# Low part of the transposed attention weights multiplied with the values' high part alone (128 columns in place of 256), in a hybrid decoder block on one core

## The chip, the cores and the metric

The kernel runs on one core of a Trainium2 chip. The metric is the device time of one execution in microseconds (us); lower is better. Five engines work side by side on a core and wait for each other by semaphores: PE (TensorE, matmuls; its weight loads are listed apart as PEld), DVE (VectorE), ACT (ScalarE), POOL (GpSimd), and SP, which here only issues DMAs.

## The reference

One decoder block over 1024 tokens of width 1024. A projection gives a pooled branch, queries, keys and values of four heads, and two gates. What the change touches is the differential attention: two softmax maps per head, one subtracted from the other, multiplied with the values.

```python
def block(args):
    qa, qb, start = args
    ...
    def probs(qq, kk):
        s = jnp.einsum('bhqd,bhkd->bhqk', qq, kk).astype(jnp.float32) * scale + bias
        s = jnp.where(causal, s, -jnp.inf)
        return jax.nn.softmax(s, axis=-1)

    a = probs(qa, k1) - lam * probs(qb, k2)
    return jnp.einsum('bhqk,bhkd->bhqd', a.astype(vh.dtype), vh)
...
m = jax.nn.sigmoid(gate_a) * ya + jax.nn.sigmoid(gate_b) * yb
h = h + rms_norm(jnp.einsum('bsd,de->bse', m, w_out), mix_post_g)
```

Everything is float32. After this comes a SwiGLU feed-forward part of 2816 hidden units, which the change leaves alone.

## The kernel before

PE multiplies in a reduced 32-bit format (fp32r), so each float32 operand is kept as two parts: `hi`, rounded, and `lo`, the rest. A product normally takes three matmuls (hi with hi, hi with lo, lo with hi): this is `triple` (lines 800 to 802). The big projections use a seven-product scheme of Strassen's kind over blocks of 512 columns.

The kernel is one program in this order: norm and projections (queries, keys, values, pooled branch, gates); the region of the mixer (function `mixer`, line 240), which holds attention, both branch products and the gating; the output projection (tiles `wo`, lines 1260 to 1262); the feed-forward part. Intermediate results go through DRAM and come back by DMA.

In the mixer, four heads times eight query blocks of 128 rows (32 rows in all) are worked off, each in three steps:

- `scores` (line 424) multiplies a query block (`QA`, `QB`: its two parts) with the keys `K` into a PSUM tile `s`, for both maps; DVE adds the distance bias and takes the minimum for the exponent (`E`, line 452), ACT takes the exponential, DVE combines the two maps into one `E` (line 466).
- `transposes` (line 471) turns each 128x128 block of `E` on PE into `aT`, up to four blocks in a PSUM bank; ACT writes the high part `AT[:, 0]` (line 484) and DVE the low part `AT[:, 1]` (line 656).
- `values` (line 492) is where the change lies. For query block `qb` it goes over key blocks `b` = 0 to `qb`. The stationary operand is a 128x128 block of `AT`, first its high part, then its low part; the moving operand is 256 columns, the 128 columns of the values' high part and beside them the 128 of their low part. Both go into 256 columns of one PSUM tile `o`. ACT takes the right half times the reciprocal of the sum (line 509), and DVE adds the left half to it (line 511), giving `O`. So the left half of `o` holds hi and lo of the weights over the values' high part, and the right half the same over the values' low part.

A head has 1+2+...+8 = 36 such blocks, four heads 144, so 288 matmuls of 256 columns.

Between these steps PE does *filler* work: the last projection products, and `block` (line 397 and after), which multiplies the branch weights (`wb_hi`, `wb_lo`) with the pooled branch (`y2h`, `y2l`; the results are copied to `ma`) or, when attention is done, with the normalised and turned attention output (`OTh`, `OTl`). For the latter the gates come by DMA into `sgs`; DVE multiplies `ma` with one half, and the block's result with the other, and adds.

The order of all this on each engine is not written by hand. `mixer` describes every step as an operation with an engine, a cost in microseconds, what it reads and writes, and a rank; `Plan.schedule` (line 144) is a list scheduler that goes through them by these costs, with the number of buffers in `CAPS` (two PSUM banks each for `mm`, which `aT` and `o` share, `fil` for branch blocks and `pair` for `s` and `oT`). The program is then issued in the planned order, and the semaphores hold the true dependencies. So a changed cost in one operation can move any operation of the region on any engine.

Of the kernel before, what the change touches and what calls it, by code (L numbers as in the profile page):

```python
# [16 lines left out]
P = 128  # L17
# [222 lines left out]
def mixer(pl, k):  # L240
# [11 lines left out]
    def bank(pool, s):  # L252
        return pl.tile(pool, lambda: getattr(k, pool)(s))
# [7 lines left out]
    def mac(o, l, r, start, stop, skip=False):  # L261
        nc.tensor.matmul(o, l, r, start=start, stop=stop, skip_group_check=skip)  # L262
# [129 lines left out]
    def block(t, hi, lo, i, mov, rank):  # L392
        o = bank("fil", "branch")
        for q in range(4):
            mh, ml = mov[q // 2]

            def fn(q=q, mh=mh, ml=ml):
                c = slice(i * P, (i + 1) * P)
                k.triple(o(), hi()[:, q, c], lo()[:, q, c], mh()[:, q % 2, half(t)], ml()[:, q % 2, half(t)],
                         q == 0, q == 3, False)  # L400
            pl.op("PE", TRIPLE, fn, r=[hi, lo, (mh, (q % 2, t)), (ml, (q % 2, t))], w=[o], rank=rank + q * .01, chain="fill")
        return o
# [6 lines left out]
    n = 0  # L409
    for d in range(0, KD, 2):  # L410
        hi, lo = branch_weights(0, d, lambda: k.w_branch_a, -3.0 + 4 * n / 3)
        for i in range(2):
            for t in range(2):
                o = block(t, hi, lo, i, y2, 2000.0 + n)
                m, c = ma[t][(d + i) // 4], (d + i) % 4
                pl.op("ACT", act(HALF), lambda m=m, c=c, o=o: A.copy(m()[:, c, :], o()), r=[o], w=[(m, c)],
                      rank=URGENT)
# [74 lines left out]
    def values(h, qb):  # L492
        Vt = heads[h][3]
        ats, rec = attends[h, qb]
        r0 = pos[h, qb]
        o = bank("mm", "o")
        for b0 in range(0, qb + 1, 4):
            n = min(4, qb + 1 - b0)

            def fn(b0=b0, n=n):  # L500
                vv = Vt().rearrange("p i (b d) -> p b i d", b=NB)
                for b in range(b0, b0 + n):
                    for j in range(2):
                        mac(o()[:, :2 * P], ats[b // 4]()[:, j, b % 4 * P:(b % 4 + 1) * P], vv[:, b, :, :],
                            b == 0 and j == 0, b == qb and j == 1)
            last = pl.op("PE", n * .24, fn, r=[ats[b0 // 4], Vt], w=[o], rank=r0)
        row_done.append(last)
        ov = lambda: O[h]()[:, qb, :]
        pl.op("ACT", .368, lambda: A.mul(ov(), o()[:, P:2 * P], rec()[:, 0:1]), r=[o, rec], w=[(O[h], qb)],
              rank=r0 - 1.5)  # L510
        pl.op("DVE", .346, lambda: V.scalar_tensor_tensor(out=ov(), in0=o()[:, :P], scalar=rec()[:, 0:1], in1=ov(),
                                                         op0=ALU.mult, op1=ALU.add), r=[o, rec],
              w=[(O[h], qb)], rank=r0 - 1.5)
        pl.op("ACT", .5, lambda: k.sumsq(ov(), oss[h]()[:, qb:qb + 1]), r=[(O[h], qb)], w=[(oss[h], qb)],
              rank=r0 - .5)
# [32 lines left out]
    for i in range(-AHEAD, len(seq)):  # L548
        j = i + AHEAD
        if j < len(seq):  # L550
            h, at = divmod(j, len(QORDER))
            if at == 2 and 0 < h < NH - 1:
                heads[h + 1] = (*load_qk(h + 1, i), *load_bv(h + 1, i))
            scores(*seq[j])
        if 0 <= i + 1 < len(seq):
            transposes(*seq[i + 1])
        if i >= 0:
            values(*seq[i])
            h, at = divmod(i, len(QORDER))
            if h < NH - 1 and at == len(QORDER) - 1:  # L560
                head_norm(h, list(range(NB)), i + 1.5)
            elif h == NH - 1 and at < NH - 1:
                for t in range(2):
                    turn_head(at, t, i + .5)
            elif h == NH - 1 and at % 4 == 3:
                head_norm(h, list(range(4, 8) if at == 3 else range(4)), i - 2.0)
                turn_head(h, 1 if at == 3 else 0, i - 1.0)
# [3 lines left out]
    for n, (d, t) in enumerate(order):  # L571
        if d not in ws:
# [4 lines left out]
        r0 = len(seq) + n  # L577
# [4 lines left out]
              r=[(sg, 0)], w=[(m, c)], rank=r0 + 2, port=True)  # L582
        if (1, d) in (k.unfinished if k else [(1, 6), (1, 7)]):
            pl.op("ACT", act(HALF) + .2, lambda sg=sg: A.activation(sg()[:, 1], sg()[:, 1], AF.Sigmoid),
                  w=[(sg, 1)], rank=r0)
        o = block(t, hi, lo, i, OT, 3000.0 + n)
        pl.op("DVE", dve(HALF), lambda o=o, sg=sg: tt(sg()[:, 1], o(), sg()[:, 1], ALU.mult), r=[o],
              w=[(sg, 1)], rank=URGENT)
        pl.op("DVE", dve(HALF), lambda m=m, c=c, sg=sg: tt(m()[:, c, :], m()[:, c, :], sg()[:, 1], ALU.add),
              r=[(sg, 1)], w=[(m, c)], rank=r0 + 1, port=True)  # L590

    wo = []
    for kp in range(4):
        hi, lo = a8([P, 2, D], F32R, "woh"), a8([P, 2, D], F32R, "wol")
        for j in range(2):
            kb = 2 * kp + j
            raw = wpt("wraw", [P, D], F32, "wo_raw")
            rank = len(seq) + 8.0 + kb
            dma(lambda raw=raw: raw(), lambda kb=kb: k.w_out[kb * P:(kb + 1) * P, :], rank, 0.52, w=[raw])
            pl.op("ACT", 1.06, lambda hi=hi, j=j, raw=raw: A.copy(hi()[:, j, :], raw()), r=[raw], w=[(hi, j)],  # L600
                  rank=rank)
            pl.op("DVE", 1.23, lambda hi=hi, lo=lo, j=j, raw=raw: k.sub(lo()[:, j, :], raw(), hi()[:, j, :]),
                  r=[raw, (hi, j)], w=[(lo, j)], rank=rank, port=True)
# [1020 lines left out]
```

## Time and profile before

| | us |
|---|---|
| median of 3 runs | 1257.43 |
| lowest and highest | 1257.41, 1257.58 |
| the profiled execution | 1257.79 |
| its span in the profile | 1255.9 |

The span runs from the first to the last instruction; 1.9 us lie around it. The granted clock of PE was 0.999 of full speed. Rows of the profile name the engine, the line of the kernel, the operation and the tiles (`o<-V,AT` writes `o` and reads `V` and `AT`), the shape and a count. In a timeline the first column is the start in microseconds from the start of the span and the second the duration; a number in square brackets is idle time of the engine ahead of the row, with what ended it. PE's matmuls overlap: what one costs in a stream is the distance from its start to the next start, not its duration.

### The profile page before, as it was taken

The numbers are of one execution on the slowest core, as the hardware profiler recorded it, in microseconds if no ns is written. First come the engines' busy times: TensorE is split into PE (matmuls) and PEld (weight loads), VectorE is DVE, ScalarE is ACT, GpSimd is POOL, SyncE is SP. The second block draws the span as 40 slices with busy tenths as digits, with TensorE's granted clock in tenths as the row PEclk, the third lists the DMA queues.
The fourth block names the chain that finished last, engine by engine and source line by source line (L and its number), as shares of the span: only waits on it lengthen the run. The fifth ranks groups of instructions, "written<-read, shape, count | busy, mean of one in ns | idle before, by whom it ended". The sixth has DMA issues, their size and how long they took to land.

```text
span 1255.9 us, 15668 instructions
## 1 busy us (share of the span) xinstructions
PE 1240.8 (99%) x5912; PEld 1040.8 (83%) x5912; DVE 835.3 (67%) x1296; ACT 578.3 (46%) x1039; POOL 144.2 (11%) x128
## 2 busy tenths in 40 slices
PE   8999999999999999999999999999999999999997
PEld 7878888888899998888888888888888888888886
DVE  5976775435498789755697655645655536965666
ACT  7543344434477774344553333333333333454552
POOL 4100000000201100010102111111111012000222
PEclk9999999999999999999999999999999999999999
DMA  8475336333692117523314332223322358733236
GB/s 253 149 233 192 138 120 224 109 122 118 233 370 102 51 51 276 177 101 118 120 57 126 126 112 98 92 95 108 126 101 88 122 195 275 250 110 106 80 108 210
DMA packets 137243, 183.34 MB, mean 146 GB/s; under 512 B 7376, under 2 KB 90064, under 8 KB 134736
## 3 DMA queue, kind: packets, MB, share of 16 engines
q1 hardware_dynamic: 124448, 147.61, 35.8%
q10 hardware_dynamic: 12720, 34.74, 7.3%
q8 instruction: 46, 0.75, 0.2%
q14 instruction: 29, 0.24, 0.1%
HBM read 124.39 MB, written 57.93 MB: 145 GB/s over the span
## 4 chain that ended last, share of the span: by engine, by line
PE 94%; DVE 2%; ACT 1%; issue 1%; POOL 1%; DMA 1%; SPq 0%; POOLq 0%; DVEq 0%; ACTq 0%
PE Y L800 10%; PE Y L801 10%; PE Y L802 10%; PE X L800 5%; PE X L801 5%; PE X L802 5%; PE Yd L800 3%; PE Yd L802 3%; PE Yd L801 3%; PE s L262 3%; PE Z L801 3%; PE Z L802 3%; PE Z L800 3%; PE o L262 3%; PE branch L800 2%; PE branch L801 2%
## 5 line engine op out<-in xcount | busy, mean ns | idle before, releaser
L729 DVE TENSOR_TENSOR p<-Z,p 128x512 f32<-128x512 f32 x34 | 23.5, 690 | 160.8 <-PE Z L802 157.1
L801 PE MATMUL Y<-A_lo,Wh 128*128 128x512 f32 x296 | 115.4, 390 | 0.3 <-DVE A_lo L656 0.3
L800 PE MATMUL Y<-A_hi,Wh 128*128 128x512 f32 x296 | 115.4, 390 | 0.0
L802 PE MATMUL Y<-A_hi,Wl 128*128 128x512 f32 x296 | 115.0, 389 | 0.0
L800 PE MATMUL Y<-S_hi,Wh 128*128 128x512 f32 x280 | 109.2, 390 | 0.7 <-ACT p L836 0.7
L800 PE MATMUL X<-S_hi,Wh 128*128 128x512 f32 x280 | 109.2, 390 | 0.0
L801 PE MATMUL Y<-S_lo,Wh 128*128 128x512 f32 x280 | 109.1, 389 | 0.0
L802 PE MATMUL Y<-S_hi,Wl 128*128 128x512 f32 x280 | 109.0, 389 | 0.0
L801 PE MATMUL X<-S_lo,Wh 128*128 128x512 f32 x280 | 108.9, 389 | 0.0
L802 PE MATMUL X<-S_hi,Wl 128*128 128x512 f32 x280 | 108.9, 389 | 0.0
L769 ACT CAST Wh<-wf_t 128x1024 fp32r<-128x1024 f32 x70 | 72.7, 1052 | 71.4 <-PE X L801 30.0
L656 DVE TENSOR_TENSOR Wl<-wf_t,Wh 128x1024 fp32r<-128x1024 f32 x70 | 87.0, 1250 | 6.2 <-ACT Wh L769 6.2
L769 ACT CAST Wh<-w_raw 128x1024 fp32r<-128x1024 f32 x72 | 60.6, 843 | 65.4 <-PE Z L801 38.1
L656 DVE TENSOR_TENSOR w_op<-wd,w_op 128x512 fp32r<-128x512 f32 x77 | 56.5, 734 | 48.4 <-ACT w_op L733 48.4
L733 ACT CAST w_op<-wd 128x512 fp32r<-128x512 f32 x77 | 47.9, 622 | 73.1 <-PE Yd L802 34.6
L656 DVE TENSOR_TENSOR Wl<-w_raw,Wh 128x1024 fp32r<-128x1024 f32 x72 | 69.1, 960 | 14.8 <-ACT Wh L769 14.7
L800 PE MATMUL Yd<-w_op,s_op 128*128 128x512 f32 x176 | 68.6, 390 | 0.0
L801 PE MATMUL Yd<-w_op,s_op 128*128 128x512 f32 x176 | 68.5, 389 | 0.0
L802 PE MATMUL Yd<-w_op,s_op 128*128 128x512 f32 x176 | 68.3, 389 | 0.0
L729 DVE TENSOR_TENSOR wf_t<-w_raw,wf_t 128x512 f32<-128x512 f32 x70 | 65.7, 938 | 1.1
L801 PEld LDWEIGHTS Y<-A_lo,Wh 128*128 128x128 f32 x296 | 55.6, 188 | 12.1 <-DVE A_lo L656 0.7
L800 PEld LDWEIGHTS Y<-A_hi,Wh 128*128 128x128 f32 x296 | 55.6, 188 | 11.8 <-DVE p L729 0.3
(274 smaller groups left out, 3055.9 us busy)
## 6 DMA issues: line engine op xcount, KB each, us to landing
s_raw<-fsd SPq DMA_DIRECT2D x35, 512.0 KB, 3.6
w_raw<-in_w_in_dram SPq DMA_DIRECT2D x32, 512.0 KB, 4.1
w_raw<-in_w_ffn_gate_dram SPq DMA_DIRECT2D x22, 512.0 KB, 3.7
w_raw<-in_w_ffn_up_dram SPq DMA_DIRECT2D x22, 512.0 KB, 3.7
fsd<-fss SPq DMA_DIRECT2D x11, 1024.0 KB, 3.9
wd<-in_w_ffn_down_dram SPq DMA_DIRECT2D x44, 256.0 KB, 5.6
fsd<-F SPq DMA_DIRECT2D x33, 256.0 KB, 2.3
qd<-qk_st ACTq DMA_DIRECT2D x16, 512.0 KB, 4.0
```

Of the source, the lines that this page charges most:

```text
L262: nc.tensor.matmul(o, l, r, start=start, stop=stop, skip_group_check=skip)
L656: nc.vector.tensor_tensor(out=o, in0=a, in1=f32(hi), op=ALU.subtract)
L729: nc.vector.tensor_tensor(out=o, in0=a, in1=b, op=op)
L733: nc.scalar.copy(hi, a)
L769: nc.scalar.copy(hi, a)
L800: nc.tensor.matmul(o, ah, bh, start=start, stop=False, skip_group_check=goes_on)
L801: nc.tensor.matmul(o, ah, bl, start=False, stop=False, skip_group_check=goes_on)
L802: nc.tensor.matmul(o, al, bh, start=False, stop=stop, skip_group_check=goes_on)
```

## The change

In `values`, the low part of the weights is multiplied with the values' high part alone. The product of the two low parts, which the right half of `o` held beside the rest, is left out. For every block after the first the narrow matmul now comes ahead of the wide one. The cost that the planner is told per block goes from 0.24 to 0.231 us, and the whole region is planned anew.

```diff
@@ -500,10 +500,10 @@
                 for b in range(b0, b0 + n):
-                    for j in range(2):
-                        mac(o()[:, :2 * P], ats[b // 4]()[:, j, b % 4 * P:(b % 4 + 1) * P], vv[:, b, :, :],
-                            b == 0 and j == 0, b == qb and j == 1)
-            last = pl.op("PE", n * .24, fn, r=[ats[b0 // 4], Vt], w=[o], rank=r0)
+                    for j in (1, 0) if b else (0, 1):
+                        mac(o()[:, :(2 - j) * P], ats[b // 4]()[:, j, b % 4 * P:(b % 4 + 1) * P],
+                            vv[:, b, :2 - j, :], b == 0 and j == 0, b == qb and j == (0 if b else 1), True)
+            last = pl.op("PE", n * .231, fn, r=[ats[b0 // 4], Vt], w=[o], rank=r0)
```

PE has as many matmuls as before; where eight of one shape stood in a row, shapes now alternate. PE's order in the first row of attention, before (`s` scores, `o` weights times values, `aT` a transpose; the numbers tell tiles apart):

```order
L262 MATMUL s_2946<-K_2155,QB_2738 128x384
L262 MATMUL o_2958<-V_2772,AT_2894 128x256 x8
L482 MATMUL aT_2970<-ident,E_2845 128x128
L262 MATMUL o_2958<-V_2772,AT_2919 128x256 x8
L262 MATMUL s_2985<-K_2155,QA_2154 128x384
```

The second half of the same row in the change:

```order
L482 MATMUL aT_2970<-ident,E_2845 128x128
L262 MATMUL o_2958<-V_2772,AT_2919 128x128
L262 MATMUL o_2958<-V_2772,AT_2919 128x256
L262 MATMUL o_2958<-V_2772,AT_2919 128x128
L262 MATMUL o_2958<-V_2772,AT_2919 128x256
L262 MATMUL o_2958<-V_2772,AT_2919 128x128
L262 MATMUL o_2958<-V_2772,AT_2919 128x256
L262 MATMUL o_2958<-V_2772,AT_2919 128x128
L262 MATMUL o_2958<-V_2772,AT_2919 128x256
L262 MATMUL s_2985<-K_2155,QA_2154 128x384
```

Each wide matmul (256 columns) now has a narrow one (128 columns) ahead of it. In the first half of the row the first block has wide ahead of narrow, and then the same pattern follows.

PE's order at the end of attention, the last three rows of head 3, before (`o_4597`, `o_4621`, `o_4637`; `oT` turns the normalised output of four rows):

```order
L262 MATMUL o_4597<-V_3845,AT_4584 128x256 x6
L538 MATMUL oT_4606<-ident,O_4344 128x128 x4
L482 MATMUL aT_4615<-ident,E_4509 128x128
L262 MATMUL o_4621<-V_3845,AT_4595 128x256 x4
L800 MATMUL branch_4541<-OTh_4489,wb_hi_4191 128x512
L801 MATMUL branch_4541<-OTl_4506,wb_hi_4191 128x512
L802 MATMUL branch_4541<-OTh_4489,wb_lo_4232 128x512
L262 MATMUL o_4637<-V_3845,AT_4619 128x256 x2
L800 MATMUL branch_4641<-OTh_4042,wb_hi_4191 128x512
```

In the change the same three rows are `o_4575`, `o_4601` and `o_4607`; what follows right behind the six matmuls of `o_4575` is:

```order
L482 MATMUL aT_4583<-ident,E_4497 128x128
L800 MATMUL branch_4585<-y2h_2746,wb_hi_3857 128x512
L801 MATMUL branch_4585<-y2l_2762,wb_hi_3857 128x512
L802 MATMUL branch_4585<-y2h_2746,wb_lo_3879 128x512
L800 MATMUL branch_4585<-y2h_2746,wb_hi_3857 128x512
L801 MATMUL branch_4585<-y2l_2762,wb_hi_3857 128x512
L802 MATMUL branch_4585<-y2h_2746,wb_lo_3879 128x512
L262 MATMUL o_4601<-V_3821,AT_4563 128x256
L262 MATMUL o_4601<-V_3821,AT_4563 128x128 x2
L262 MATMUL o_4601<-V_3821,AT_4563 128x256
L262 MATMUL o_4607<-V_3821,AT_4593 128x256
L262 MATMUL o_4607<-V_3821,AT_4593 128x128
```

Between the third last and the second last row there is now one transpose and half a block of the pooled branch, where the `oT` transposes stood; a whole block of the pooled branch has been kept for this place, and the first block over the attention output comes after all rows.

DVE's order around the second pair of branch weights over the attention output (`wb_lo`, read from the third such block on), before:

```order
L543 TENSOR_SCALAR OTl_4506<-oT_4491,sgc,OTh_4489 128x512
L511 TENSOR_SCALAR O_4344<-o_4497,rec_4318,O_4344 128x128
L656 TENSOR_TENSOR AT_4525<-aT_4483,AT_4525 128x512
L452 ISA E_4509,nm_4523<-s_4531,negd_2716 128x128
L452 ISA nm_4523 128x1
L656 TENSOR_TENSOR wb_lo_4563<-wb_raw_3814,wb_hi_4545 128x1024
```

And in the change:

```order
L265 TENSOR_TENSOR ma_3231<-ma_3231,sgs_4514 128x512
L543 TENSOR_SCALAR OTl_4481<-oT_4568,sgc,OTh_4469 128x512
L511 TENSOR_SCALAR O_4330<-o_4575,rec_4395,O_4330 128x128
L656 TENSOR_TENSOR AT_4593<-aT_4583,AT_4593 128x128
L265 TENSOR_TENSOR ma_3231<-ma_3231,sgs_4553 128x512
L511 TENSOR_SCALAR O_4330<-o_4601,rec_4458,O_4330 128x128
L511 TENSOR_SCALAR O_4330<-o_4607,rec_4544,O_4330 128x128
L521 TENSOR_SCALAR ms_4637<-oss_2709 128x4
L265 TENSOR_TENSOR ma_3231<-ma_3231,sgs_4590 128x512
L656 TENSOR_TENSOR wb_lo_4659<-wb_raw_3928,wb_hi_4646 128x1024
```

The weights' low part now stands behind the last rows of attention and behind three multiplications with gates that DMAs bring (`sgs`); before it stood ahead of all of them.

## The prediction

> **What bounds the kernel now.** I began with the page: busy times and the chain of waits.
>
> ```profile
> PE 1240.8 (99%) x5912; PEld 1040.8 (83%) x5912; DVE 835.3 (67%) x1296; ACT 578.3 (46%) x1039; POOL 144.2 (11%) x128
> PE 94%; DVE 2%; ACT 1%; issue 1%; POOL 1%; DMA 1%; SPq 0%; POOLq 0%; DVEq 0%; ACTq 0%
> ```
>
> PE is busy 99% of the span and carries 94% of the chain. A matmul's modelled end lies behind the next start, so busy hides small waits; the list of PE's own waits over the whole execution and busy time by stage tell more. The stages are the mixer's beginning, middle, late part, its tail of 6 us, the blocks over the attention output, and the output projection.
>
> ```profile
> PE o L262 <- DVE O L511: 0.5, 1, 0.5
> PE h_t L1403 <- DVE og L1397: 0.7, 1, 0.7
> ```
>
> ```profile
> core 0: us, PE busy (x) PEld busy (x) DVE busy (x) ACT busy (x) POOL busy (x), PEclk, DMA share, GB/s
> 340.00:400.00 60.00, 60.00 (x366) 53.75 (x366) 55.49 (x151) 45.31 (x125) 4.01 (x2) 1.00 0.75 282
> 400.00:440.00 40.00, 40.00 (x252) 36.11 (x251) 31.04 (x81) 28.38 (x83) 4.06 (x2) 1.00 0.11 41
> 440.00:476.00 36.00, 36.00 (x240) 32.90 (x239) 32.26 (x82) 28.86 (x77) 2.23 (x2) 1.00 0.14 45
> 476.00:482.00 6.00, 5.47 (x33) 4.43 (x32) 5.87 (x14) 3.73 (x14) 0.97 (x1) 1.00 0.70 227
> 482.00:522.00 40.00, 40.00 (x180) 33.13 (x179) 38.08 (x58) 14.45 (x20) 1.01 (x1) 1.00 0.80 282
> ```
>
> In the mixer PE sets the end. It idles in one place alone, 0.53 us in the tail, waiting for DVE. Work taken off PE in this region is therefore time taken off the kernel, as long as DVE, 92% busy in the first stage (55.49 of 60) and 95% in the fifth, keeps up in the new order.
>
> **The change, part by part: the narrow matmuls.** 144 of the 288 wide matmuls become narrow. What a wide one costs now, and a 128-column transpose, is read from the chain, where runs stand merged (start, length, what):
>
> ```profile
> 384.95 1.92 PE o L262 x16
> 414.91 0.87 PE aT L482 x8
> ```
>
> A wide one takes 1.92 / 16 = 0.120 us, and 0.1195 is what I use, since other runs are a little shorter; a transpose takes 0.109. No narrow matmul alternates with wide ones before. The nearest row is the score of the first query block, two narrow fp32r matmuls between 512-column ones, with the weight loads between them:
>
> ```profile
> 341.42 0.22 PE L262 MATMUL s<-K,QA 128*128 128x128 f32 x1
> 341.42 0.19 PEld L262 LDWEIGHTS s<-K,QB 128*128 128x128 f32 x1
> 341.48 0.28 PE L262 MATMUL s<-K,QB 128*128 128x128 f32 x1
> 341.53 0.19 PEld L800 LDWEIGHTS X<-S_hi,Wh 128*128 128x128 f32 x1
> 341.59 0.45 PE L800 MATMUL X<-S_hi,Wh 128*128 128x512 f32 x1
> 341.64 0.19 PEld L801 LDWEIGHTS X<-S_lo,Wh 128*128 128x128 f32 x1
> 341.88 0.39 PE L801 MATMUL X<-S_lo,Wh 128*128 128x512 f32 x1
> 342.11 0.39 PE L802 MATMUL X<-S_hi,Wl 128*128 128x512 f32 x1
> ```
>
> The start behind the first narrow one comes after 0.06 us, but the 512-column matmul behind the pair then needs 0.29 in place of 0.23 (341.88 to 342.11). From 341.42 to 341.88 the three take 0.46, so the two narrow ones cost 0.23 together, 0.115 each. The loads say why: they start 0.11 us apart (341.42, 341.53, 341.64). A narrow matmul streams for about half of that, and the next one waits for its weights. A wide one hides the next load whole. So a narrow one costs what a load costs: between 0.109 (the transposes' row) and 0.115 (this pair). The saving per block lies between 0.1195 - 0.115 = 0.0045 and 0.1195 - 0.109 = 0.0105 us, for 144 blocks between 0.6 and 1.5 us. In the new order each narrow one stands next to a wide one, which hides the load ahead of it, so one load per block is exposed; I take the loads' own distance of 0.11: 0.0095 x 144 = **1.4 us**.
>
> The Trainium skill, page "TensorE: Matmul & The Clock Gate", section "Back-to-back issue gap", has N/2.4 + 2.5 ns for one matmul in a stream, which is 56 ns for 128 columns; its section "LDWEIGHTS (loading the stationary operand)" has columns/1.2, which is 107 ns for 128 columns. By the first a block would save some 64 ns and all blocks 9.1 us, by the second 13 ns and 1.8 us. The trace's load distance of 0.11 us sides with the second, and the page itself adds that its formula is too low at small N where loads count.
>
> That the narrow one comes first from the second block on makes the fifth block's first matmul wait for DVE's low part, where before it waited for ACT's high part only, and DVE's followed one matmul (0.12 us) later. Cover for it: between the transposes and the values of a row stand microseconds of scores and filler. Without that cover it costs up to 0.12 for each of the 16 rows with a second group, 1.9 us; I take 0.
>
> **The new order: the tail.** Here lies PE's only idle time. PE, ACT and DVE before:
>
> ```profile
> 477.07 0.98 PE L262 MATMUL o<-V,AT 128*128 128x256 f32 x6
> 477.88 0.60 PE L538 MATMUL oT<-ident,O 128*128 128x128 f32 x4
> 478.09 0.37 ACT L509 ACTIVATE O<-o,rec 128x128 f32<-128x128 f32 x1 [0.42 <-PE o L262]
> 478.21 0.68 DVE L265 TENSOR_TENSOR ma<-ma,sgs 128x512 f32<-128x512 f32 x1
> 478.35 0.33 PE L482 MATMUL aT<-ident,E 128*128 128x128 f32 x1
> 478.81 0.34 DVE L511 SCALAR_TENSOR_TENSOR O<-o,rec,O 128x128 f32<-128x128 f32 x1
> 479.21 0.74 PE L262 MATMUL o<-V,AT 128*128 128x256 f32 x4 [0.53 <-DVE O L511]
> 480.05 0.50 PE L801 MATMUL branch<-OTl,wb_hi 128*128 128x512 f32 x1
> 480.85 0.40 PE L800 MATMUL branch<-OTh,wb_hi 128*128 128x512 f32 x1
> ```
>
> The four matmuls at 479.21 need the PSUM bank of the six at 477.07, and that is free when ACT and then DVE have read it; DVE does a gate multiplication first. From 477.07 to 480.85 pass 3.78 us. The work in it is 6 + 4 + 2 wide (12 x 0.1195 = 1.43), 5 transposes (0.55) and 3 branch matmuls. One of these takes 0.227: the output projection has 42 from its first to its last key block, in 531.67 - 522.15 = 9.52 us.
>
> ```profile
> 522.15 0.39 PE L1260 MATMUL wo<-woh,mh 128*128 128x512 f32 x1
> 531.67 0.39 PE L1260 MATMUL wo<-woh,mh 128*128 128x512 f32 x1
> 526.86 1.22 DVE L656 TENSOR_TENSOR wol<-wo_raw,woh 128x1024 fp32r<-128x1024 f32 x1 [0.54 <-ACT woh L600]
> ```
>
> Together 2.66, so the tail loses 1.12 us. Between the same rows the new order has one transpose and six branch matmuls, 0.109 + 6 x 0.227 = 1.47 us of cover; what it has to cover is 479.21 - 477.79 (477.07 and six wide) = 1.42 if DVE is as late as before. But DVE now also has an `OTl` piece (0.75 like its kin) ahead of that eviction, begun earlier. Between 0 and 1.12 come back; nearer the upper end, since 1.47 covers 1.42, less a remainder of about 0.3 for `OTl`: **0.8 us**. The last row finds its bank free since the same filler.
>
> **The new order: the rest.** Work does not change in amount. Two moved pieces touch a queue: in SP's order head 3's keys now stand behind a branch weight, which waits until POOL has read the weight buffer; and head 3's first scores come earlier, by some 7 us of PE work.
>
> ```profile
> 386.95 2.41 POOL L386 TENSOR_TENSOR wb_lo<-wb_raw,wb_hi 128x1024 fp32r<-128x1024 f32 x1 [51.30 <-PE o L262]
> 435.47 0.40 PE L262 MATMUL s<-K,QA 128*128 128x512 f32 x1
> ```
>
> POOL is done at 389.36 and the scores would start at about 428.5: 39 us for loads that land within 12. This costs nothing. Behind the mixer nothing eats the gain: the output projection's last weights are ready at 526.86 + 1.22 = 528.1 and read at 531.67, 3.6 us of slack against a start about 2 us earlier. Elsewhere I expect no new wait, and price that at 0 with a loss of up to 1 us left open: one wait like the one of 0.53 or two.
>
> **Sum.** 1.4 + 0.8 = 2.2 us off the profiled execution's 1257.79 gives 1255.6; the median of the runs lies 0.36 under that execution, so 1257.43 - 2.2 = **1255.2**. Own range of this case: 0.6 + 0 to 1.5 + 1.1, less up to 0.5 of new waits, so 1254.8 to 1256.8.
>
> **Rivals.**
>
> *Only the narrow part comes.* The list scheduler makes waits as chance has it; the new order has new ones for the old. DVE's load of 92 to 95% speaks for it, PE's single wait in 150 us against. Then 1.4 remain: 1256.0.
>
> *Slower: the third gate load holds the branch weights.* In the new order DVE writes `wb_lo_4659` behind the multiplication with the third gate tile, and the third block over the attention output reads it. Before:
>
> ```profile
> 474.58 1.22 DVE L656 TENSOR_TENSOR wb_lo<-wb_raw,wb_hi 128x1024 fp32r<-128x1024 f32 x1 [0.33 <-ACT wb_hi L384]
> 476.31 14.72 SPq L349 DMA_DIRECT2D sgs<-sgd  x14
> 481.69 0.69 DVE L265 TENSOR_TENSOR ma<-ma,sgs 128x512 f32<-128x512 f32 x1
> 482.79 0.69 DVE L265 TENSOR_TENSOR ma<-ma,sgs 128x512 f32<-128x512 f32 x1 [0.15 <-DMA sgs<-sgd]
> DMA to landing us min/median/max: 4.1/10.4/11.7
> ```
>
> The third load was asked for at 476.31 and used, without a wait, at 481.69; loads land after 4.1 to 11.7 us. In the new order the third block's start lies 14 blocks of 12 matmuls, 168 x 0.227 = 38.1 us, ahead of the output projection's, which would be 522.15 - 2.2 = 519.95: at 481.8. DVE needs 0.69 + 1.22 before it, so the load must land by 479.9. Each us behind that is a us on PE; from 482.1 the gain is gone, from 484.6 the kernel is slower by over 0.2%. If it is asked for at 476.31 and lands after 11.7, at 488.0, PE waits 8.1: 1263.3. Against it: SP asks for it right behind the second, no longer behind a weight that waits for DVE, so earlier than 476.31 and into idle DMA queues.
>
> *Loads do not limit.* If the queue pulls loads far enough ahead, a narrow one costs the 0.06 between the first two starts of the pair: 144 x 0.0595 = 8.6, with the tail 9.4: 1248.0. The 0.29 behind the pair speaks against it. (This is what the Trainium skill's formula for one matmul in a stream, named above, would come to here.)
>
> *The change does not do what it says.* A narrow one costs as much as a wide one, 0.1195, if a change of shape costs a few ns each time; 0.115 in the pair is near it. Then the tail alone is left: 1256.6.
>
> **How the numbers follow.** Forecast 0.61, only the narrow part 0.16, slower 0.10, no saving per block 0.08, loads free 0.05. The range of 1254.3 to 1257.2 holds the first, second and fourth with their bounds and leaves out the slower one and the free loads. A change under 0.2%, 2.5 us, is about what a measurement of this kernel can't tell from none. 2.2 is close to that: of the forecast's 0.61 I give 0.18 to over 2.5 (both upper bounds, 1.5 + 1.1, make 2.6). Faster 0.18 + 0.05 = 0.23; slower 0.08, the part of its case that lands behind 484.6; within 0.69.
>
> **What would show it.** In the changed profile: runs of `o` with one narrow and one wide matmul per 0.23 us, and weight loads no closer than 0.11; PE's idle time at the second last row gone or under 0.3; no wait of PE for `wb_lo` or DMA at the third block; the output projection's first matmul at 519.9 in place of 522.15, and the same distance from there to the end. It is wrong if a pair takes 0.24 or 0.18, if the list of PE's waits has new rows in the mixer, or if the gain is lost behind it.

## The result, and the profile after

| | before | after |
|---|---|---|
| median, us | 1257.43 (19 runs, 1257.25 to 1257.95) | 1255.21 (19 runs, 1254.88 to 1255.52) |
| the profiled execution, us | 1257.79 | 1255.21 |
| its span, us | 1255.9 | 1253.4 |

The ratio of after to before is 0.9982, with a 95% interval of 0.9975 to 0.9989. The change saves 2.22 us, 0.18%. The interval leaves out 1, so the gain is real, but it is below the 0.2% that the prediction put as the bound for a faster kernel.

PE is still what bounds the kernel. The page of the changed kernel, busy time by engine:

```profile
PE 1239.6 (99%) x5912; PEld 1040.0 (83%) x5912; DVE 836.2 (67%) x1296; ACT 579.4 (46%) x1039; POOL 144.1 (11%) x128
```

As many matmuls as before, and only 1.2 us less of busy time; since a matmul's modelled end lies behind the next start, this figure is not the gain. The list of PE's own waits in the changed kernel (total, times, longest, in us):

```profile
PE x_t L952 <- DVE xt L924: 2.9, 2, 1.5
PE k L942 <- POOL ident masks.py:199: 1.4, 1, 1.4
PE q L676 <- DVE A_lo L656: 1.3, 2, 0.8
PE h_t L1403 <- DVE og L1397: 0.7, 1, 0.7
PE Y L800 <- ACT p L836: 0.7, 1, 0.7
PE Y L801 <- DVE A_lo L656: 0.3, 1, 0.3
PE x_t L952 <- ACT A_raw L968: 0.2, 1, 0.2
```

The row `PE o L262 <- DVE O L511: 0.5` of before is gone, and none of the rows that are left lies in the mixer. The first row stands at the program's beginning, ahead of everything that was changed; it varies by itself, 3.7 in the profile of before and between 2.3 and 3.4 in the four kernels further down that have the wide matmul first in some or all blocks and do the same work there.

The first scores of attention and the output projection's first matmul in the changed kernel (timeline: start, duration):

```profile
341.07 0.22 PE L262 MATMUL s<-K,QA 128*128 128x128 f32 x1
519.67 0.39 PE L1260 MATMUL wo<-woh,mh 128*128 128x512 f32 x1
```

It was at 522.15, so 2.48 us have been won up to here, of 2.5 in the span. Of these, 0.35 lie ahead of the first scores, which were at 341.42 and are now at 341.07: that is the program's beginning, which the change does not touch. The two profiled executions lie 2.58 us apart and the medians 2.22, and these 0.35 are the difference. Between the first scores and the output projection 180.73 us have become 178.60, a gain of 2.13. From the output projection to the end pass 1253.4 - 519.67 = 733.7 us, before 1255.9 - 522.15 = 733.75. Nothing is lost or won behind the mixer.

A row of eight key blocks in the chain of the changed kernel (start, length, what; the two other rows of this form take as long):

```profile
385.00 1.85 PE o L262 x16
```

Sixteen matmuls take 1.85 where they took 1.92. A pair of one narrow and one wide matmul costs 1.85 / 8 = 0.231 us in place of 0.240; the difference, 0.07 / 8 = 0.0088 us, is 1.26 us for 144 blocks. Taken instruction by instruction, the starts of the matmuls in such a row lie 0.06 and 0.17 us apart in turn, and the starts of their weight loads 0.11 and 0.12.

The end of attention in the timeline of the changed kernel, from the six matmuls of the third last row on:

```profile
471.22 0.68 DVE L265 TENSOR_TENSOR ma<-ma,sgs 128x512 f32<-128x512 f32 x1
471.33 0.94 PE L262 MATMUL o<-V,AT 128*128 128x256 f32 x6
472.10 0.27 PE L482 MATMUL aT<-ident,E 128*128 128x128 f32 x1
472.30 0.37 ACT L509 ACTIVATE O<-o,rec 128x128 f32<-128x128 f32 x1
472.38 0.75 DVE L543 SCALAR_TENSOR_TENSOR OTl<-oT,sgc,OTh 128x512 fp32r<-128x512 f32 x1 [0.48 <-ACT OTh L541]
473.05 0.34 DVE L511 SCALAR_TENSOR_TENSOR O<-o,rec,O 128x128 f32<-128x128 f32 x1
473.37 0.40 PE L802 MATMUL branch<-y2h,wb_lo 128*128 128x512 f32 x1
473.60 0.81 PE L262 MATMUL o<-V,AT 128*128 128x256 f32 x6
```

The bank of `o` comes free when DVE ends its eviction, at 473.05 + 0.34 = 473.39. Only at 473.60, when the filler ends, does PE turn to the next row (two rows of attention, six matmuls, follow each other there). The cover is 0.21 us longer than what it covers, and PE has no idle time in front of it.

### The profile page after: what moved, and what is told of

The parts are those of the page before. It is cut to its first block, busy times and chain, and to the rows that moved or that the text cites. A ratio compares the mean times of both kernels' runs of the same rounds, so it can differ in the third digit from the quotient of the medians.

```text
span 1253.4 us, 15675 instructions
## 1 busy us (share of the span) xinstructions
PE 1239.6 (99%) x5912; PEld 1040.0 (83%) x5912; DVE 836.2 (67%) x1296; ACT 579.4 (46%) x1039; POOL 144.1 (11%) x128
## 4 chain that ended last, share of the span: by engine, by line
PE 94%; DVE 2%; ACT 1%; issue 1%; POOL 1%; DMA 1%; SPq 0%; POOLq 0%; DVEq 0%; ACTq 0%
PE Y L800 10%; PE Y L801 10%; PE Y L802 10%; PE X L802 5%; PE X L800 5%; PE X L801 5%; PE Yd L800 3%; PE Yd L802 3%; PE Yd L801 3%; PE s L262 3%; PE Z L802 3%; PE Z L801 3%; PE Z L800 3%; PE o L262 3%; PE branch L800 2%; PE branch L802 2%
## 5 line engine op out<-in xcount | busy, mean ns | idle before, releaser
L769 ACT CAST Wh<-w_raw 128x1024 fp32r<-128x1024 f32 x72 | 60.6, 843 | 65.5 <-PE Z L801 38.1
L801 PEld LDWEIGHTS Y<-A_lo,Wh 128*128 128x128 f32 x296 | 55.6, 188 | 12.1 <-DVE A_lo L656 0.7
```

The lines of the kernel that those rows point to most:

```text
L769: nc.scalar.copy(hi, a)
L801: nc.tensor.matmul(o, ah, bl, start=False, stop=False, skip_group_check=goes_on)
```

## The experiments

The ratios are against the kernel before as it was measured beside each run, 1257.43 us for the first four runs and for the last three, 1257.58 for the three between. Two things were changed at once: the width of a matmul, and the order of the whole region. The first two runs separate them.

**Narrow matmuls in the order of before** (`e1_narrow_old_order`), an edit to the changed kernel:

```diff
-            last = pl.op("PE", n * .231, fn, r=[ats[b0 // 4], Vt], w=[o], rank=r0)
+            last = pl.op("PE", n * .24, fn, r=[ats[b0 // 4], Vt], w=[o], rank=r0)
```

> The narrow matmuls in the order of before (the planner is told 0.24 per block, so every engine's order is that of before). Theory (two separate terms: about 1.2 us from the matmuls, about 1 us from the tail that the new order lost): PE's wait in the tail stays near 0.5 us, a wide and a narrow one together take 0.231 in place of 0.239, and the time is 1256.1 to 1256.4. Rival (the narrow matmul costs as much as the wide one, and the order gave all): 1257.4. Rival (the matmuls gave all, the order nothing): 1255.2.

Measured: 1256.32 us (11 runs, 1256.16 to 1256.72), ratio 0.9990 [0.9981, 0.9999]. This is 1.11 less than before, and no run of the one reaches into the range of the other. The row of eight blocks in its chain and the wait in its tail (timeline):

```profile
384.53 1.84 PE o L262 x16
```

```profile
477.59 0.35 DVE L511 SCALAR_TENSOR_TENSOR O<-o,rec,O 128x128 f32<-128x128 f32 x1
477.99 0.73 PE L262 MATMUL o<-V,AT 128*128 128x256 f32 x4 [0.53 <-DVE O L511]
```

The narrow matmuls alone bring about half of the gain, and the 0.53 us wait of before stands where it stood, at its old length.

**Wide matmuls in the new order** (`e2_wide_new_order`), an edit to the kernel before:

```diff
-            last = pl.op("PE", n * .24, fn, r=[ats[b0 // 4], Vt], w=[o], rank=r0)
+            last = pl.op("PE", n * .231, fn, r=[ats[b0 // 4], Vt], w=[o], rank=r0)
```

> The wide matmuls of before in the new order (the planner is told 0.231 per block). Theory: PE's wait in the tail is gone with the order alone, and the 144 wide ones cost their 1.2 us more: 1256.3 to 1256.5. Rival (the order gave all): 1255.2. Rival (the order gives nothing, the tail's wait was due to the longer matmuls): 1257.4.

Measured: 1256.16 us (11 runs, 1256.01 to 1256.34), ratio 0.9989 [0.9981, 0.9998], 1.27 less than before, with its row at the old price and no wait for `O`:

```profile
385.09 1.91 PE o L262 x16
```

One number in the planner's table, with no change to what is computed, is worth as much as taking a quarter of the products away from 144 blocks. Both parts together: 1.11 + 1.27 = 2.38 beside the 2.22 measured for the change. They add up. The traces say the same without the program's beginning: from the first scores to the output projection the narrow matmuls alone win 0.88 us (341.18 to 521.03), the order alone 1.12 (340.93 to 520.54), together 2.00 beside 2.13.

**Half of the narrow matmul's columns** (`e3_half_narrow`). Is it the stream of columns that a narrow matmul pays for, or the load of its weights?

```diff
-                    for j in (1, 0) if b else (0, 1):
-                        mac(o()[:, :(2 - j) * P], ats[b // 4]()[:, j, b % 4 * P:(b % 4 + 1) * P],
-                            vv[:, b, :2 - j, :], b == 0 and j == 0, b == qb and j == (0 if b else 1), True)
+                    for j, w in ((1, P // 2), (0, P)) if b else ((0, P), (1, P // 2)):
+                        mac(o()[:, :(2 - j) * w], ats[b // 4]()[:, j, b % 4 * P:(b % 4 + 1) * P],
+                            vv[:, b, :2 - j, :w], b == 0 and j == 0, b == qb and j == (0 if b else 1), True)
```

> The new kernel with the narrow matmuls halved once more, to 64 columns; half of the columns of the product of low weights and high values is left out. Theory (a narrow matmul costs the load of the next weights, 0.11 us, however few columns it streams): the pair stays at 0.231 and the time at 1255.2, within 0.3. Rival (it costs its columns plus something fixed): 64 columns at 2.4 per ns are 0.027 us less each, 144 times 3.8 us: 1251.4.

Measured: 1254.83 us (11 runs, 1254.6 to 1255.09), ratio 0.9979 [0.9970, 0.9988]. Its groups of instructions over the mixer show the narrow ones at 64 columns, and its chain the row:

```profile
L262 PE MATMUL o<-V,AT 128*128 128x64 f32 x144 | 25.5, 209 | 0.0
```

```profile
384.59 1.82 PE o L262 x16
```

64 columns less saved 0.38 us in all, slightly more than the 0.3 that was allowed for, and 0.38 / 144 = 2.6 ns each. The wide matmul at 0.1195 for 256 columns would put 64 columns at 30 ns, so nine tenths of what was taken out of the stream was not on the path. So the columns do not set what a narrow matmul costs. Nor does a fixed distance of 0.11 us between matmuls: in the row of the changed kernel every second start follows after 0.06. What keeps a distance of 0.11 there are the weight loads.

**No narrow matmul at all** (`e4_no_low`), which takes the load away as well:

```diff
-                    for j in (1, 0) if b else (0, 1):
-                        mac(o()[:, :(2 - j) * P], ats[b // 4]()[:, j, b % 4 * P:(b % 4 + 1) * P],
-                            vv[:, b, :2 - j, :], b == 0 and j == 0, b == qb and j == (0 if b else 1), True)
+                    mac(o()[:, :2 * P], ats[b // 4]()[:, 0, b % 4 * P:(b % 4 + 1) * P], vv[:, b, :, :],
+                        b == 0, b == qb)
```

> The new kernel without the narrow matmuls; the product of the low weights with the values is left out, the low weights are still made. The order is the new one. This gives the price of a narrow matmul by itself. Theory: 144 times 0.112 is 16.1 us if PE stays the bound: 1239.1, less what DVE (92 to 95% busy in parts of this region) then gives back as waits: 1239 to 1246, with new rows in the list of PE's waits, all on DVE or ACT. Rival (the price is the columns' 0.056): 8 us, 1247.2 and no new waits.

Measured: 1245.02 us (4 runs, 1244.93 to 1245.08), ratio 0.9900 [0.9887, 0.9914]. That is 10.2 us less than the change, where 144 x (0.231 - 0.1195) would be 16.1. PE's waits in this kernel that the change has not, and its busy times by stretch (PE, PEld, DVE, ACT, POOL, then granted clock, DMA share and GB/s):

```profile
PE aT L482 <- DVE O L511: 0.9, 3, 0.4
PE aT L482 <- DVE AT L656: 0.5, 2, 0.3
```

```profile
340.00:400.00 60.00, 59.18 (x340) 50.45 (x339) 58.31 (x162) 48.94 (x139) 4.05 (x2) 1.00 0.79 295
400.00:440.00 40.00, 39.36 (x233) 34.01 (x232) 38.80 (x100) 34.14 (x94) 4.00 (x2) 1.00 0.05 14
```

DVE is busy 58.31 of 60 and 38.80 of 40 us, 97% in both. The waits listed come to 1.4 us of the missing 5.9. The chain of this kernel shows the rest: of the pieces between 340 and 509 us, where the mixer ends here, 84 us lie on DVE (its bias and minimum, `E` of line 452, most of all) and 81 on PE, where the chain of the change has nothing but PE in this region. So the work left on PE for these 144 matmuls is worth at least 10 us, but DVE stands close behind PE and sets an end to it.

**Another cost for the planner** (`e5_cost_228` and `e6_cost_2305`). Is the new order a good one, or does any new order bring such a gain? The computation is that of the change in both:

```diff
-            last = pl.op("PE", n * .231, fn, r=[ats[b0 // 4], Vt], w=[o], rank=r0)
+            last = pl.op("PE", n * .228, fn, r=[ats[b0 // 4], Vt], w=[o], rank=r0)
```

> The new matmuls, but the planner is told 0.228 per block in place of 0.231: a third order, with the same work. In it the blocks of the pooled branch are used up early (three stand in a row ahead of the last rows of head 2), and the last 24 us of attention have hardly any filler left; four places there leave 0.2 to 0.65 us of PE work between two uses of a PSUM bank, where the order before left 0.55 in one and paid 1.1 us. Theory (a small change of a cost draws another order, and what it is worth lies in the waits of that order): PE waits in many places late in attention, 5 to 15 us in all: 1260 to 1270. Rival (PE is the bound, so any order of the same work takes about the same): 1254.9 to 1255.9.

Measured: 1269.72 us (4 runs, 1268.72 to 1270.82), ratio 1.0095 [1.0082, 1.0109]: slower than before by 12.1 us, and than the change by 14.5. PE's waits in the mixer of this kernel, and the two stretches in which they lie:

```profile
PE o L262 <- DVE AT L656: 2.5, 1, 2.5
PE s L262 <- DVE nm L452: 2.2, 4, 1.0
PE o L262 <- DVE O L511: 0.5, 1, 0.5
PE aT L482 <- DVE AT L656: 0.4, 1, 0.4
PE aT L482 <- DVE E L466: 0.3, 1, 0.3
```

```profile
440.00:476.00 36.00, 31.11 (x149) 23.37 (x147) 26.70 (x60) 23.81 (x54) 1.64 (x1) 0.95 0.09 30
476.00:500.00 24.00, 22.39 (x140) 19.25 (x141) 22.01 (x55) 11.30 (x39) 2.11 (x2) 1.00 0.74 252
```

In the late part PE has run out of filler, so that the chain from scores over DVE and ACT to the next matmul lies open: PE idles 4.89 of 36 and 1.61 of 24 us. That is 6.5 of the 13.5 us that part the two profiled executions, but idle time does not hold all of it: of the chain's pieces between 440 and 500 us 20 lie on DVE and 34 on PE, where the chain of the change has nothing but PE. In the first of the two stretches the granted clock was 0.95 as well, where it is 1.00 in the others shown; what that adds while DVE sets the pace is not known.

The same edit with 0.2305 in place of 0.228 gave the second kernel.

> The new matmuls with 0.2305 in place of 0.231 per block: an order that is the new one up to head 2 or so and differs at the end; the shortest cover of a PSUM bank in its tail is 1.1 to 1.2 us where the new one has 1.47. Theory (a wait comes where cover falls under about 1.4, the time that ACT and DVE took in the tail of before): one or two waits of up to 0.3 us, 1255.2 to 1255.7. Rival (the tail has no wait): 1255.2 or a little less.

Measured: 1255.24 us (11 runs, 1254.97 to 1255.53), ratio 0.9981 [0.9972, 0.9989], the time of the change. No wait in the mixer was found; the thinner covers of this order still sufficed. So the gain from the order is neither a property of any new order nor of this one alone: of three orders from costs within 1.3% of each other, two are worth about 1.1 us and one costs 13.4, each beside the same matmuls in the order of before (1256.32).

**The wide matmul first** (`e7_wide_first`). The change puts the narrow matmul ahead of the wide one from the second block on. With the wide one first everywhere:

```diff
-                    for j in (1, 0) if b else (0, 1):
+                    for j in (0, 1):
...
-                            vv[:, b, :2 - j, :], b == 0 and j == 0, b == qb and j == (0 if b else 1), True)
+                            vv[:, b, :2 - j, :], b == 0 and j == 0, b == qb and j == 1, True)
```

> The new order with the wide matmul ahead of the narrow one in every block, so that a second group of blocks starts as soon as ACT's high part is there. Theory (each narrow one exposes one load wherever it stands, and DVE's part is there long before): 1255.2, within 0.2. Rival (that the narrow one stands first costs a wait for DVE's low part in the 16 rows with a second group): up to 1.9 us less, 1253.3.

Measured: 1254.63 us (10 runs, 1254.28 to 1255.00), ratio 0.9976 [0.9967, 0.9986]; 0.58 less than the change. Neither kernel has a wait of PE in the mixer, so a wait for DVE's low part, the cause that the rival named, was not what the change paid for. Nor does the theory hold that the place of the narrow one makes no difference: 0.58 is more than the 0.2 that it allowed. A row of eight blocks in its chain is shorter (the two others take 1.78 and 1.80):

```profile
384.37 1.80 PE o L262 x16
```

Two things differ from the change within a row: its start (the change has two narrow ones behind each other, of the first and the second block) and its end (a wide one in the change, a narrow one here). Two runs on one chip took them apart.

**The wide one first in the first and last block of a row alone** (`e8_last_block_wide_first`): the row ends narrow, and the pair of narrow ones at its start stays.

```diff
-                    for j in (1, 0) if b else (0, 1):
+                    for j in (0, 1) if b in (0, qb) else (1, 0):
...
-                            vv[:, b, :2 - j, :], b == 0 and j == 0, b == qb and j == (0 if b else 1), True)
+                            vv[:, b, :2 - j, :], b == 0 and j == 0, b == qb and j == 1, True)
```

> The change with one difference: in the last block of a row of blocks (and in the first, as before) the 256-column matmul of the high part comes ahead of the 128-column one; all other blocks stand as in the change, the narrow one first. So every row ends with a narrow matmul, and the two narrow ones that follow each other at a row's start stay. Theory: what made the run with the wide one first in every block 0.58 us faster is the row's end (a 128-column transpose behind a narrow matmul costs about 0.055 us less than behind a wide one, some 11 rows in which one follows): 1254.6, and the row of eight blocks ahead of transposes takes 1.80 in place of 1.85. Rival: it is the row's start or the blocks' inner order (the pair of narrow matmuls at the start gone): then this run is the change's, 1255.2, and the row takes 1.85.

**The wide one first in all but the last block** (`e9_last_block_narrow_first`): the row ends wide, and no narrow ones stand together at its start.

```diff
-                    for j in (1, 0) if b else (0, 1):
+                    for j in (1, 0) if b and b == qb else (0, 1):
```

> The opposite of the run beside it: the wide matmul first in every block but the last of a row, where the narrow one comes first, so that every row ends with a wide matmul and no narrow ones follow each other at its start. Theory (the row's end sets the gain): none of the 0.58 us, 1255.2, with 1.85 for a row of eight blocks ahead of transposes. Rival (the row's start or the inner order sets it): 1254.6, with 1.80.

Measured: 1254.55 us (10 runs, 1254.49 to 1254.80), ratio 0.9977 [0.9968, 0.9986], for the one that ends narrow; 1255.09 us (11 runs, 1254.82 to 1255.37), ratio 0.9981 [0.9972, 0.9990], for the one that ends wide. The ranges do not meet. The end of the row decides, and neither its start nor the order inside. What stands behind a row decides too. The change's second row of eight blocks has transposes behind it, the first one scores of 320 columns; timelines of both (each the row, and what follows; the first score behind the transposes is left out):

```profile
384.84 2.02 PE L262 MATMUL o<-V,AT 128*128 128x256 f32 x16
386.69 0.31 PE L262 MATMUL s<-K,QA 128*128 128x320 f32 x1
386.84 0.31 PE L262 MATMUL s<-K,QB 128*128 128x320 f32 x1
...
416.19 2.02 PE L262 MATMUL o<-V,AT 128*128 128x256 f32 x16
418.05 0.60 PE L482 MATMUL aT<-ident,E 128*128 128x128 f32 x4
418.63 0.31 PE L262 MATMUL s<-K,QB 128*128 128x320 f32 x1
```

The same in the kernel whose rows end narrow (`e8_last_block_wide_first`):

```profile
384.36 1.95 PE L262 MATMUL o<-V,AT 128*128 128x256 f32 x16
386.15 0.37 PE L262 MATMUL s<-K,QA 128*128 128x320 f32 x1
386.36 0.31 PE L262 MATMUL s<-K,QB 128*128 128x320 f32 x1
...
415.63 1.95 PE L262 MATMUL o<-V,AT 128*128 128x256 f32 x16
417.42 0.61 PE L482 MATMUL aT<-ident,E 128*128 128x128 f32 x4
418.02 0.31 PE L262 MATMUL s<-K,QB 128*128 128x320 f32 x1
```

Ahead of scores both take the same to the second score: 386.84 - 384.84 = 2.00 and 386.36 - 384.36 = 2.00. The row is shorter by 0.06 and the score behind it longer by as much. Ahead of transposes a part stays won: 418.63 - 416.19 = 2.44 beside 418.02 - 415.63 = 2.39. The weight loads show where. Those of the four transposes behind the third row of eight blocks, in the change and in the kernel whose rows end narrow:

```profile
453.32 0.46 PEld L482 LDWEIGHTS aT<-ident,E 128*128 128x128 f32 x4
452.66 0.42 PEld L482 LDWEIGHTS aT<-ident,E 128*128 128x128 f32 x4
```

Behind a wide matmul the load after the first one starts 0.10 us later, behind a narrow one 0.06. Attention has 13 rows that end ahead of such transposes, and all 13 show this, read instruction by instruction: 0.096 to 0.104 in the change and 0.093 to 0.100 in the other kernel whose rows end wide, 0.045 to 0.059 in the one whose rows end narrow. At 0.04 for each, 13 rows make about the 0.54 between the two runs. Why the load can start earlier there was not tried.

**The wide one first, in the order for 0.2305** (`e10_wide_first_2305`): `e7_wide_first` with the cost of `e6_cost_2305`. Against the former:

```diff
-            last = pl.op("PE", n * .231, fn, r=[ats[b0 // 4], Vt], w=[o], rank=r0)
+            last = pl.op("PE", n * .2305, fn, r=[ats[b0 // 4], Vt], w=[o], rank=r0)
```

> The wide matmul first in every block, with the order that the scheduler makes for a cost of 0.2305 for a block in place of 0.231. Sought: a version faster than the one with the wide matmul first in the change's order (1254.63). Theory: the order for 0.2305 left no stall in the mixer and the same time as the change's (1255.24 beside 1255.21), so this one comes to 1254.6 as well, within 0.3. Rival: the shorter row brings a new wait in this order, whose covers were the thinner ones (1.09 to 1.23 us for a 0.8 us chain): 1255.0 or more, with a wait of PE for DVE's O, AT or nm in the mixer.

Measured: 1254.59 us (11 runs, 1254.52 to 1254.92), ratio 0.9978 [0.9969, 0.9987], without a wait in the mixer. The three kernels whose rows end narrow, 1254.55, 1254.59 and 1254.63, cannot be told apart; each is some 0.6 us faster than the change and 2.8 to 3.0 us faster than before.

## Why the prediction was right, step by step

The forecast was 1255.2, and 1255.21 was measured. That it comes out to 0.01 is chance: two terms were off by little and on opposite sides, and the prediction's own range ran from 1254.8 to 1256.8.

- *A narrow matmul costs what a load costs.* Right. The pair costs 0.231, so the narrow one 0.231 - 0.1195 = 0.1115 beside the 0.11 that the prediction took, and inside its bounds of 0.109 and 0.115. The run with 64 columns shows that the columns are not the reason, and the loads' distances in the row, 0.11 and 0.12, side with the load. The Trainium skill, page "TensorE: Matmul & The Clock Gate", section "LDWEIGHTS (loading the stationary operand)", has columns/1.2 ns, by which 128 columns are estimated at 107 ns, and the trace's 0.1115 us lies within 5 ns of that; its section "Back-to-back issue gap" gives about 81 ns as the measured distance of matmuls with N=128 that each have a load of their own, and here the trace disagrees, with 0.1115 for the narrow matmuls and 0.109 for the transposes.
- *The term of 1.4 us.* A little too large: 1.26 by the rows, 1.11 by the times of the run that has the narrow matmuls alone, 0.88 between its first scores and its output projection.
- *The tail, 0.8 us.* Right as to the cover: one transpose and six branch matmuls cover the eviction, and the wait is gone. Its size was taken too small. The 0.3 set aside for the `OTl` piece on DVE was not lost: DVE had ended the gate multiplication at 471.90, waited 0.48 for ACT, and was through with `OTl` and the eviction 0.21 ahead of PE. The new order by itself measured 1.27 by the times and 1.12 between first scores and output projection, the whole 1.12 that the tail was said to lose. What the prediction did not follow is why DVE was late before. The chain of before leaves PE at 473.47 and comes back at 479.21 (start, length; parts left out at the dots):

```profile
473.49 1.06 ACT wb_hi L384
474.58 1.22 DVE wb_lo L656
...
478.89 0.27 DVE O L511
479.21 0.74 PE o L262 x4
```

  So the wait of 0.53 is the end of 5.7 us of work on ACT and DVE that begins with the branch weights' high and low part. The new order moves that pair behind the last rows of attention, and it puts more work of PE between the rows; how much each of the two is worth no run tells.
- *The new order elsewhere, 0.* Right: no row of the wait list lies in the mixer. That was no safe ground. The order for a cost of 0.228 has five such rows and costs 12 us more than before, and the prediction had put at most 1 us on new waits of this sort (its own range takes off only 0.5, and its upper end of 1256.8 leaves even that out: 0.6 + 0 less 0.5 would be 1257.3).
- *The fifth block's narrow matmul ahead of the wide one, 0.* Right as to waits: none for DVE's low part appears. But the order of the two has a price that the prediction did not see, at the row's other end: 0.5 to 0.6 us.
- *Only the narrow part comes (1256.0).* This is what the kernel with the old order does, 1256.32, and not what the change does.
- *The third gate load holds the branch weights (1263.3).* It did not. DVE's rows around it in the changed kernel:

```profile
476.00 0.68 DVE L265 TENSOR_TENSOR ma<-ma,sgs 128x512 f32<-128x512 f32 x1
477.42 1.23 DVE L656 TENSOR_TENSOR wb_lo<-wb_raw,wb_hi 128x1024 fp32r<-128x1024 f32 x1 [0.74 <-ACT wb_hi L384]
```

  The multiplication with the third gate ran at 476.00 without waiting for a DMA, where the prediction allowed the load until 479.9, and what `wb_lo` waited for was ACT. It was done at 478.65, 3 us ahead of the third block, which by the prediction's distance of 38.1 us from the output projection begins at 481.6. The loads had been asked for early, as the argument against this rival had it: the third by 464.7, where it was 476.31 before.
- *Loads do not limit (1248.0).* Refuted by the pair's 0.231 and by the 2.6 ns that 64 columns were worth.
- *The change does not do what it says (1256.6).* Refuted by the pair's 0.231 in place of 0.240, and by the kernel with the narrow matmuls alone: 1.11 us, with an interval that leaves out 0, if barely (0.9999).
- *What would show it.* The first matmul of the output projection at 519.9: it was at 519.67 (at 520.0 without the 0.35 of the program's beginning), and the distance to the end is the same as before. Loads no closer than 0.11: so it is within the rows, while the first two loads of the transposes behind a row come 0.10 apart.

## What to carry to other kernels

A matmul of 128 columns with weights of its own cost about as much as the load here, 0.11 us, so halving a 256-column matmul of 0.12 saved less than a tenth of it; to save more, the load itself has to go, and with it went 10 us. Where a planner sets the order, test an edit apart from the order that it brings, by giving the old code the new order and the new code the old one: here each was worth half. And when both have been found good, try costs a per cent off and the two ways round inside the loop: the first shows how near a bad order is, and the second brought another 0.6 us.

## What the runs showed of the hardware that was not expected

- A row that ends in a 128-column matmul and is followed by 128-column transposes takes 0.05 us less than one that ends in a 256-column matmul (2.39 in place of 2.44 us from its start to the second score behind it), with the same matmuls in it. Followed by matmuls of 320 columns it takes the same. The weight loads at that place start 0.06 us apart, so 0.11 is not the least distance between two loads.
- A matmul of 64 columns costs only 2.6 ns less than one of 128 where each alternates with a 256-column matmul.
